# Gate/up of a two-layer encoder: where the second half's norm scales are spread, and three sums and products moved from GpSimd to VectorE

## The chip, the cores and the metric

The kernel runs on one core of a Trainium2 chip. A core has TensorE (PE, matrix products into PSUM), VectorE (DVE), ScalarE (ACT), GpSimd (POOL), and SyncE (SP), which here issues the DMA transfers. Each engine works through its own queue in order; semaphores tie the queues together. The metric is the device time of one execution in microseconds (us); less is better.

## The reference, cut to what matters

The reference is an encoder trunk of two layers over 1024 tokens of width 1024, all in fp32. The part that the change touches is the second half of each layer, the gated feed-forward:

```python
h = rms_norm(x, g_ffn[l]) * (1 + sc_f) + sh_f
gate, up = split_cols(h @ w_gu[l], (FFN_HIDDEN, FFN_HIDDEN))
x = x + gt_f * ((jax.nn.silu(gate) * up) @ w_down[l])
```

`FFN_HIDDEN` is 2816, so the gate and up matrices have 22 column blocks of 128 each. `rms_norm` divides each token by the root of the mean square of its 1024 features, so a token's scale is known only when all eight feature blocks of `x` are final.

## The kernel before, in words

**Tiling.** `x` lies transposed in SBUF: eight blocks `xt[:, k, :]` of 128 features by 1024 tokens (tiles `xb`, tags `x0` to `x7`). Tokens are taken in two halves of 512. Every fp32 factor is split into a high part (an fp32r copy by ACT) and a low part (the difference, by DVE or POOL), and a product is the sum of three matrix products of such parts (`mm3`, L202).

**Strassen-like products.** The 1024 by 256 weight columns of one step and the two halves of `h` are cut in 2 by 2, and seven products replace eight (`PRODUCTS`, L218: numbers 1, 2, 6, 5, 7, 3, 4, on operands `h11, h21, ht2, ht1, ht3, h22, ht4`). Each is 12 matmuls of 128x512 (`product`, L278). They accumulate in three PSUM banks per step: 1, 6, 7 and 4 in bank "a", 2 in "b", 5 and 3 in "c". Between two products of one bank ACT copies out what stands in it, so the second has to wait for that copy. `gu_product` (L1862) runs one product and what follows: ACT copies (`take`), DVE adds PSUM (`add`), and the gate's silu (ACT) or the multiplication by up (`done`).

**Steps.** There are 22 steps `q`, gate (even) and up (odd) in turn; two make a column block pair. The results of a pair lie in two tiles `sg`, which take the places of `x4` and `x5` for the first pair and `x6` and `x7` for the second (`gu_start`, L1942; `x_tile`, L1829). So the first results can be written only when the last reader of those blocks of `x` is through.

**The early loop.** Products 1 and 2 need only the first half of the tokens. The second half's norm is not ready when gate/up begins, so the first seven steps run products 1 and 2 first (`EARLY = 7`, L1956; the loop at L1994). In it `rstd_rows` (L458) is taken forward by two `next(norm)`: the first, at q = 0, sums the squares over features with PE and takes root and reciprocal; the second, at q = 1, spreads the scales over the partitions by four PE transposes into a PSUM tile `ps_r` (`spread`, L449) and returns it as `rows`. From q = 1 to 4, `t2_part` (L1961) multiplies two blocks of `x` by `rows` (`h_norm`, L1769) and makes `ht2` and `ht1`; `t3_part` and `t4_part` (L1978, L1983) make `ht3`, `h22` and `ht4`. All of that is DVE work with ACT copies between.

**The late loop** (L2017) then runs products 6, 5, 7, 3, 4 of steps 0 to 6, and all seven of the later steps. Weights come by DMA (`wr`, `gu_raw` L1832), are combined into sums (`ws`) by DVE and split (`wpt`) by ACT with DVE or POOL, up to eight ahead (`Ahead`, L261). The loads of step 1 and the sums use the places of `x0` to `x3`. The first ten splits are DVE's; after that DVE and POOL take turns.

**What sets the order.** Except for SP's queue, which is held in program order in the late loop (`pin`, L2016), the instructions are put in order for each engine by the compiler's planner: it takes the earliest in program order among those that its own clock holds ready. So an engine's order isn't the program's where a wait leaves room; in the trace, TensorE runs half of product 4 of step 0 ahead of product 3.

The line of the profile is always L49 (a wrapper that issues every instruction); instructions are told apart by the tiles they write and read.

Of the kernel before, what the change touches and what calls it, by code (L numbers as in the profile page):

```python
# [14 lines left out]
ALU = mybir.AluOpType  # L15
# [70 lines left out]
def trunk(ctx: ExitStack, tc, A, C, out):  # L86
    nc = tc.nc
    pe, act, dve, pool, sp = (
        Engine(tc, e) for e in (nc.tensor, nc.scalar, nc.vector, nc.gpsimd, nc.sync)
    )  # L90
# [187 lines left out]
    def product(num, banks, bank, a, b, m):  # L278
        if num in (1, 2, 5):
            banks[bank] = psl.tile([P, 512], F32, name="ps_w", tag="mm")  # L280
        ps = banks[bank]
        for k in range(m):
            mm3(
                ps, a[0][:, k], a[1][:, k], b[0][:, k], b[1][:, k],
                num in (1, 2, 5) and k == 0, k == m - 1, skip_group_check=True,
            )
        return ps
# [161 lines left out]
    def spread(r, j0, psp, tag="mm"):  # L449

        ps = psp.tile([P, 512], F32, name="ps_r", tag=tag)
        for j in range(4):
            pe.transpose(
                ps[:, j * P : (j + 1) * P], bc(r[:, j0 + j : j0 + j + 1], [P, P]), ident
            )
        return ps

    def rstd_rows(ssq, ntp, psp):  # L458

        r = rstd_cols([ssq], D, 4, ntp, psp)  # L460
        yield
        yield spread(r, 0, psp)
# [334 lines left out]
    rows = spread(rxs[1], 0, psl)  # L797
# [21 lines left out]
    for l in range(2):  # L819
# [175 lines left out]
        norm = {}  # L995
# [175 lines left out]
        for oc in range(NE, 8):  # L1171
            w = wab
            for half in range(2):
# [15 lines left out]
                i = 2 * (oc - NE) + half  # L1189
# [407 lines left out]
        for n in range(-AHEAD - 1, N + 1):  # L1597
# [44 lines left out]
            for end, (chunks, width) in norms.items():  # L1642
                if begins[end] <= m <= end and (m - begins[end]) % 8 == 7:
                    i = (m - begins[end]) // 8
# [150 lines left out]
        for i, n in enumerate((6, 7, 0, 1, 2, 3, 4, 5)):  # L1795
# [9 lines left out]
            if i == 1:  # L1805
                norm = rstd_rows(ssq, ntp, psl)
                next(norm)
            if i == 3:
                rows = next(norm)
# [22 lines left out]
        def gu_raw(q):  # L1832

            b, up = q // 2, q % 2
            c0 = up * FF + 2 * b * P
            raws = []
            for i in range(2):
                if q % 2:
                    t = x_tile(2 + i, [P, 4, 2 * P], "wr")
                else:  # L1840
                    t = wp.tile([P, 4, 2 * P], F32, name="wr", tag="wst", bufs=2)
                src = w_gu[:, c0 : c0 + 2 * P].rearrange("(k h p) n -> h p k n", h=2, p=P)
                sp.dma_start(t, src[i])
                raws.append(t)
            return raws
# [14 lines left out]
        sg, quads = {}, {}  # L1860

        def gu_product(q, p, a):  # L1862
            num, b, bank = p
            up = q % 2
            t = quads.setdefault(q, {})
            ps = product(num, t, bank, a, hb[b], 4)
            e, o = sg.get(q // 2, (None, None))
            lo, hi = slice(0, H), slice(H, S)

            def take(key, out=None):  # L1870
                if num == 1 and 5 <= q < EARLY:
                    out = spare[:, (q - 5) * H : (q - 4) * H]
                if out is None:
                    tag, bufs = ("u4", 1) if (q, num) == (4, 1) else ("u", 4)
                    out = ffp.tile([P, H], F32, name="u", tag=tag, bufs=bufs)
                t[key] = out
                act.copy(out, ps)

            def add(key):
                dve.tensor_tensor(out=t[key], in0=t[key], in1=ps, op=ALU.add)  # L1880

            def done(dst, src, eng=dve):
                if up:
                    eng.tensor_tensor(out=dst, in0=dst, in1=src, op=ALU.mult)
                else:
                    act.activation(dst, src, AF.Silu)

            if num == 1:
                take("11")
            elif num == 2:  # L1890
                add("11")
                if e is not None:
                    done(e[:, lo], t["11"], pool)
            elif num == 6:
                take("12", None if up else e[:, hi])
            elif num == 5:
                take("22", None if up else o[:, hi])
            elif num == 7:
                take("x")
                t22 = t["22"]  # L1900
                pool.tensor_tensor(out=t22, in0=t22, in1=t["x"], op=ALU.add)
                done(o[:, hi], t["22"], pool)
            elif num == 3:
                add("12")
                done(e[:, hi], t["12"], pool)
            else:
                done(o[:, lo], ps)
                if up:
                    steps.append(g_steps(q // 2, e, o))
# [3 lines left out]
        def g_steps(b, e, o):  # L1913


            b11, b12, b21, b22 = (t[:, i * H : (i + 1) * H] for t in (e, o) for i in range(2))

            def put(name, src):
                sp.dma_start(gpd[:, PLACE[name] + b, :], src)

            due = {
                3: lambda: [put(*a) for a in (("11", b11), ("22", b22), ("21", b21))],
                8: lambda: sub(b11, b12, b11),
                9: lambda: (sub(b12, b22, b12), sub(b22, b22, b11), put("t1", b11)),
                10: lambda: sub(b21, b21, b22),
                11: lambda: (put("t3", b12), put("t2", b22)),
                12: lambda: put("t4", b21),
            }
            return [due.get(i, lambda: None) for i in range(13)]
# [12 lines left out]
        def gu_start(b):  # L1942
            g_finish(1)
            sg[b] = [x_tile(4 + 2 * (b % 2) + i, [P, S], "sg") for i in range(2)]


        def first_cols(c0):
            rows = w_gu[:, c0 : c0 + P].rearrange("(k h p) n -> h p k n", h=2, p=P)
            return split_w(
                lambda v: [(v[:, 4 * i : 4 * i + 4], rows[i]) for i in range(2)], KC, eng=dve  # L1950
            )
# [9 lines left out]
        def t2_part(i, rows):  # L1961


            k = 2 * i
            for j in range(2):
                h_norm(k + j, 1, rows)
            b11, b12, b21, b22 = (
                xt[:, k + j, m * H : (m + 1) * H] for j in range(2) for m in range(2)
            )
            tag, bufs = ("ssq", 1) if i == 3 else ("sq", 2)  # L1970
            t2 = ntp.tile([P, H], F32, name="t2", tag=tag, bufs=bufs)
            sub(b11, b12, b11)
            shifted_sub(t2, b22, shift(k + 1), b11)
            h_split("t2", i, t2, dve)
            h_split("t1", i, b11, dve)
            return b12, b21, b22, t2

        def t3_part(i, b12, b21, b22, t2):  # L1978

            shifted_sub(b12, b22, dsh[:, i : i + 1], b12)  # L1980
            h_split("t3", i, b12, dve)

        def t4_part(i, b12, b21, b22, t2):  # L1983

            h_shift_split("22", i, b22, shift(2 * i + 1))
            shifted_sub(b21, b21, shift(2 * i + 1), t2)
            h_split("t4", i, b21, dve)
# [3 lines left out]
        rows = None  # L1991
        norm = rstd_rows(ssq, ntp, psl)
        ahead = Ahead(gu_parts())
        for q in range(EARLY):  # L1994
            for i in range(2):
                a = [w[:, 4 * i : 4 * i + 4] for w in early[q]]
                gu_product(q, PRODUCTS[i], a)
            if q + 4 < EARLY:
                early.append(first_cols((q + 4) % 2 * FF + (q + 4) // 2 * 2 * P))
            elif raw0 is None:  # L2000
                raw0 = gu_raw(0)
            if q == 0:
                next(norm)
            if q == 1:
                rows = next(norm)
            if 1 <= q < 5:
                bs.append(t2_part(q - 1, rows))
            if q == 1:
                t3_part(0, *bs[0])
                t4_part(0, *bs[0])  # L2010
            if q == EARLY - 2:
                ahead.fill(5)
# [4 lines left out]
        for q in range(NF):  # L2017
            if q % 2 == 0:
                gu_start(q // 2)
            if q < EARLY:  # L2020
                up = q % 2
                e = sg[q // 2][0][:, 0:H]
                if up:
                    pool.tensor_tensor(out=e, in0=e, in1=quads[q]["11"], op=ALU.mult)
            for i, p in enumerate(PRODUCTS[2 if q < EARLY else 0 :]):
                gu_product(q, p, ahead.get())
                if i == 1 and q < EARLY and not up:
                    act.activation(e, quads[q]["11"], AF.Silu)
                ahead.fill()
                g_step()  # L2030
                if q >= EARLY:
                    next(mods_due, None)
# [167 lines left out]
        for u in range(NU):  # L2200
            i, t = divmod(u, NB)
# [69 lines left out]
        norm = norm_half(odd, 1)  # L2271
# [91 lines left out]
```

## Time and profile before

| what | value |
|---|---|
| median of 3 runs | 2432.55 us (2431.05 to 2435.31) |
| the profiled execution's own time | 2435.83 us |
| its span, first to last instruction | 2434.1 us |
| PE busy | 2362.9 us (97%) |
| DVE busy | 1785.1 us (73%) |
| ACT busy | 1203.9 us (49%) |
| POOL busy | 759.6 us (31%) |
| mean granted TensorE clock | 0.991 |
| gate/up of layer 0, first product | at 589.09 us of the span |
| late loop of layer 0, first product | at 628.59 us |
| late loop of layer 1, first product | at 1815.16 us |

How to read it: the times in the rows of a timeline are from the start of the span. A row gives start, duration, engine, operation, the tile written and the tiles read, and in brackets how long the engine stood idle before it and what released it. With "x2" a row holds two instructions in a row. The end of a matmul is modelled, and matmuls overlap, so their pace is read from starts.

### The profile page before, as it was taken

The page shows a single profiled execution, that of the slowest core. Times are in us where ns is not written, and L with a number is a line of the kernel's source. Part 1 is how long each engine was busy: PE and PEld are TensorE (multiplying, and loading weights), DVE is VectorE, ACT ScalarE, POOL GpSimd, SP SyncE. Part 2 cuts the span into 40 slices and gives each one's busy share as a digit, 9 for nine tenths or more (in the row PEclk, how much of TensorE's full clock was granted, in tenths as well). Part 3 has the DMA queues.
Part 4 walks back from the last instruction along what each step waited for, and adds up shares of the span by engine and source line. Part 5 has one row for each costly group of instructions (what it writes and reads, how often), then busy time and mean ns, then how long its engine had stood idle before and what let it go on. Part 6 is the DMA issues. An engine that isn't in the chain of part 4 may idle for free.

```text
span 2434.1 us, 33735 instructions
## 1 busy us (share of the span) xinstructions
PE 2362.9 (97%) x11733; PEld 1963.3 (81%) x11733; DVE 1785.1 (73%) x2950; ACT 1203.9 (49%) x2290; POOL 759.6 (31%) x741
## 2 busy tenths in 40 slices
PE   8999999999999999999999999999999999999998
PEld 5778888788788788788787879987877888888886
DVE  5756899976967788586677589998787545547865
ACT  3421788954543333344543148887454333334443
POOL 1530344620244444300036114464004444430001
PEclk9999999999999999999999999999999999999999
DMA  8478215154245454596434861242534422329643
GB/s 262 151 237 269 61 27 148 43 181 148 87 143 178 156 183 150 166 276 195 144 96 113 277 187 27 58 125 68 191 96 136 142 100 96 103 101 305 206 129 108
DMA packets 305338, 356.98 MB, mean 147 GB/s; under 512 B 51964, under 2 KB 221788, under 8 KB 305168
## 3 DMA queue, kind: packets, MB, share of 16 engines
q1 hardware_dynamic: 283296, 342.07, 44.5%
q10 hardware_dynamic: 21504, 12.59, 2.0%
q8 instruction: 93, 1.52, 0.3%
q14 instruction: 77, 0.63, 0.1%
q0 software_dynamic: 368, 0.17, 0.0%
HBM read 269.79 MB, written 88.63 MB: 147 GB/s over the span
## 4 chain that ended last, share of the span: by engine, by line
PE 50%; DVE 4%; issue 4%; ACT 2%; POOL 1%; DMA 1%; ACTq 0%; SPq 0%; POOLq 0%; DVEq 0%
PE ps_w L49 21%; PE ps_d L49 14%; PE ps_o L49 3%; PE pv L49 2%; PE ps_ab L49 2%; PE ps_v L49 2%; PE T L49 2%; PE sC L49 2%; DMA qkd<-qko 1%; ACT pr L49 1%; PE ps_c L49 1%; POOL ct L49 1%; DVE pt L49 0%; PE ps_st L49 0%; DVE pr L49 0%
## 5 line engine op out<-in xcount | busy, mean ns | idle before, releaser
L49 PE MATMUL ps_d<-wpt 128*128 128x512 f32 x1848 | 424.3, 390 | 2.2 <-ACT wpt L49 1.9
L49 PEld LDWEIGHTS ps_d<-wpt 128*128 128x128 f32 x1848 | 345.6, 188 | 76.2 <-issue 3.0
L49 POOL TENSOR_SCALAR pr<-pr,rs 128x1024 f32<-128x1024 f32 (+2 forms) x248 | 192.8, 780 | 228.8 <-DVE rs L49 203.2
L49 POOL TENSOR_TENSOR sg<-sg,u 128x512 f32<-128x512 f32 x86 | 125.8, 1465 | 356.5 <-ACT sg L49 117.9
L49 PE MATMUL pv<-pt,vs 128*128 128x256 f32 x1088 | 182.5, 296 | 10.8 <-DVE y L49 3.6
L49 ACT CAST wpt<-w 128x512 fp32r<-128x512 f32 x154 | 95.7, 621 | 179.9 <-PE ps_d L49 161.4
L49 DVE TENSOR_TENSOR pt<-T,pt 128x512 fp32r<-128x512 f32 x272 | 178.2, 681 | 6.9 <-ACT pt L49 5.1
L49 PE MATMUL T<-identr,pr 128*128 128x128 f32 x1176 | 172.8, 273 | 1.0 <-DVE pt L49 0.5
L49 ACT CAST pt<-T 128x512 fp32r<-128x512 f32 x272 | 153.0, 586 | 37.8 <-PE T L49 35.8
L49 ACT COPY u<-ps_w 128x512 f32<-128x512 f32 x128 | 75.1, 587 | 193.1 <-PE ps_w L49 192.9
L49 POOL TENSOR_TENSOR wpt<-ws,wpt 128x512 fp32r<-128x512 f32 x80 | 112.3, 1405 | 179.0 <-ACT wpt L49 132.5
L49 DVE TENSOR_TENSOR wpt<-w,wpt 128x512 fp32r<-128x512 f32 x154 | 108.9, 707 | 80.6 <-ACT wpt L49 78.4
L49 PEld LDWEIGHTS pv<-pt,vs 128*128 128x128 f32 x1088 | 145.3, 189 | 27.6 <-DVE y L49 9.8
L49 PEld LDWEIGHTS T<-identr,pr 128*128 128x128 f32 x1176 | 138.2, 140 | 18.3 <-POOL pr L49 1.3
L49 DVE SCALAR_TENSOR_TENSOR acc<-wmt,condT,acc 128x512 f32<-128x512 f32 (+1 forms) x98 | 116.9, 1201 | 44.2 <-DMA wmt<-in_w_mod_dram 43.7
L49 ACT CAST wpt<-ws 128x512 fp32r<-128x512 f32 x176 | 107.7, 622 | 63.4 <-issue 28.2
L49 DVE TENSOR_TENSOR wpt<-ws,wpt 128x512 fp32r<-128x512 f32 x96 | 82.3, 868 | 62.9 <-ACT wpt L49 62.8
L49 DVE TENSOR_TENSOR wpt<-graw,wpt 128x512 fp32r<-128x512 f32 x154 | 109.2, 709 | 19.3 <-ACT wpt L49 19.3
L49 ACT CAST wpt<-graw 128x512 fp32r<-128x512 f32 x154 | 95.0, 617 | 48.2 <-DMA graw<-gpd 40.3
L49 DVE TENSOR_TENSOR ws<-wr 128x512 f32<-128x512 f32 x88 | 80.0, 911 | 49.2 <-POOL wpt L49 46.0
L49 PE MATMUL ps_w<-h22h,wpt 128*128 128x512 f32 x352 | 111.6, 399 | 4.3 <-ACT sg L49 3.6
L49 DVE TENSOR_REDUCE rs<-sC 128x1 f32<-128x1024 f32 x88 | 107.1, 1218 | 7.1 <-PE sC L49 5.2
(299 smaller groups left out, 6024.5 us busy)
## 6 DMA issues: line engine op xcount, KB each, us to landing
wr<-in_w_gu_dram SPq DMA_DIRECT2D x92, 512.0 KB, 4.1
gpd<-sg SPq DMA_DIRECT2D x154, 256.0 KB, 4.4
graw<-gpd SPq DMA_DIRECT2D x76, 512.0 KB, 3.5
w<-in_w_down_dram SPq DMA_DIRECT2D x110, 256.0 KB, 5.4
wmt<-in_w_mod_dram SPq DMA_DIRECT2D x48, 512.0 KB, 6.1
qk<-qkd SPq DMA_DIRECT2D x44, 512.0 KB, 6.7
wst<-in_w_o_dram SPq DMA_DIRECT2D x32, 512.0 KB, 3.9
wmt<-in_w_mod_dram SPq DMA_DIRECT2D x64, 256.0 KB, 3.8
```

The lines of the kernel that those rows point to most:

```text
L49: ins = op(*args, **kwargs)
```

## The change

The second `next(norm)` of the early loop moves from behind step 1's two products (and the load of a later step's first weights) to between them. And three elementwise operations of steps 0 and 1 (128x512 each) go to DVE in place of POOL: the sum that follows product 7 in steps 0 and 1 (`t22 + x`), and the multiplication of step 1's product "11" into `e`, the gate's silu. The same operations of steps 2 and on stay on POOL.

```diff
@@ gu_product
             elif num == 7:
                 take("x")
                 t22 = t["22"]
-                pool.tensor_tensor(out=t22, in0=t22, in1=t["x"], op=ALU.add)
+                (pool if q > 1 else dve).tensor_tensor(out=t22, in0=t22, in1=t["x"], op=ALU.add)
                 done(o[:, hi], t["22"], pool)
@@ early loop
             for i in range(2):
                 a = [w[:, 4 * i : 4 * i + 4] for w in early[q]]
                 gu_product(q, PRODUCTS[i], a)
+                if q == 1 and i == 0:
+                    rows = next(norm)
             if q + 4 < EARLY:
                 early.append(first_cols((q + 4) % 2 * FF + (q + 4) // 2 * 2 * P))
             elif raw0 is None:
                 raw0 = gu_raw(0)
             if q == 0:
                 next(norm)
-            if q == 1:
-                rows = next(norm)
             if 1 <= q < 5:
                 bs.append(t2_part(q - 1, rows))
@@ late loop
                 up = q % 2
                 e = sg[q // 2][0][:, 0:H]
                 if up:
-                    pool.tensor_tensor(out=e, in0=e, in1=quads[q]["11"], op=ALU.mult)
+                    (pool if q > 1 else dve).tensor_tensor(
+                        out=e, in0=e, in1=quads[q]["11"], op=ALU.mult
+                    )
```

## The prediction

> **What bounds the kernel now.** I read the page's first part, then the waits of TensorE over both gate/up stages, then the timelines of PE, DVE, ACT and POOL around those waits, and the granted clock there.
>
> ```profile
> span 2434.1 us, 33735 instructions
> PE 2362.9 (97%) x11733; PEld 1963.3 (81%) x11733; DVE 1785.1 (73%) x2950; ACT 1203.9 (49%) x2290; POOL 759.6 (31%) x741
> ```
>
> PE bounds the kernel as a whole, so the change can only win where PE stands or runs slowly. In layer 0's gate/up it stands three times (from 573 to 720 us), all at one place; layer 1 answers with the same three:
>
> ```profile
> PE ps_w L49 <- ACT sg L49: 2.6, 2, 1.8
> PE ps_w L49 <- ACT u L49: 0.9, 1, 0.9
> ```
>
> The PE timeline shows the place: the late products of step 0.
>
> ```profile
> 628.59 0.62 PE L49 MATMUL ps_w<-ht2h,wpt 128*128 128x512 f32 x2
> ...
> 631.31 0.69 PE L49 MATMUL ps_w<-ht1h,wpt 128*128 128x512 f32 x2
> ...
> 635.07 0.74 PE L49 MATMUL ps_w<-ht3h,wpt 128*128 128x512 f32 x2 [0.79 <-ACT sg L49]
> ...
> 639.05 0.72 PE L49 MATMUL ps_w<-ht4h,wpt 128*128 128x512 f32 x2 [0.92 <-ACT u L49]
> ...
> 642.26 0.73 PE L49 MATMUL ps_w<-h22h,wpt 128*128 128x512 f32 x2 [1.79 <-ACT sg L49]
> ...
> 648.33 0.39 PE L49 MATMUL ps_w<-ht2h,wpt 128*128 128x512 f32 x1
> ...
> 1815.16 0.62 PE L49 MATMUL ps_w<-ht2h,wpt 128*128 128x512 f32 x2
> ...
> 1836.08 0.40 PE L49 MATMUL ps_w<-ht2h,wpt 128*128 128x512 f32 x1
> ```
>
> One product takes 631.31 - 628.59 = 2.72 us at full pace. Five of them from 628.59 would let step 1 begin at 642.19; it begins at 648.33, 6.14 late. Layer 1: 1815.16 + 13.60 = 1828.76, in fact 1836.08, 7.32 late. So 13.46 us in both layers is all that a cure of this place can bring. Part of it is the clock (columns: window, length, busy us of PE, PEld, DVE, ACT, POOL, granted clock, DMA share, GB/s):
>
> ```profile
> 640.00:645.00 5.00, 3.21 (x12) 2.27 (x11) 4.91 (x6) 1.84 (x3) 2.16 (x2) 0.86 0.92 302
> 645.00:650.00 5.00, 5.00 (x19) 3.93 (x19) 4.16 (x8) 3.65 (x7) 0.00 (x0) 0.80 0.37 121
> 1827.00:1832.00 5.00, 3.21 (x9) 2.48 (x9) 4.88 (x7) 1.83 (x3) 1.72 (x2) 0.60 0.93 309
> 1832.00:1837.00 5.00, 5.00 (x17) 3.98 (x16) 3.08 (x6) 2.97 (x6) 0.00 (x0) 0.72 0.35 110
> ```
>
> Lost by it: 5 x (0.14 + 0.20) = 1.7 us in layer 0, 5 x (0.40 + 0.28) = 3.4 in layer 1. The rest is waiting.
>
> ACT is only the last link of those waits. Its copies into `sg` wait for DVE, the last reader of the blocks of `x` that `sg` replaces:
>
> ```profile
> 634.43 0.59 ACT L49 COPY sg<-ps_w 128x512 f32<-128x512 f32 x1 [0.64 <-DVE ht3l L49]
> 635.04 1.28 ACT L49 ACT_TABLE_LOAD   x1
> ...
> 641.62 0.59 ACT L49 COPY sg<-ps_w 128x512 f32<-128x512 f32 x1 [2.63 <-DVE ht4l L49]
> ```
>
> And DVE is behind from the moment the norm scales arrive:
>
> ```profile
> 596.72 0.17 DVE L49 RECIPROCAL rstd<-rstd 128x4 f32<-128x4 f32 x1
> 601.19 0.69 DVE L49 TENSOR_TENSOR u<-u,ps_w 128x512 f32<-128x512 f32 x1 [4.30 <-PE ps_w L49]
> 601.79 0.74 DVE L49 SCALAR_TENSOR_TENSOR xb<-xb,gsc,ps_r 128x512 f32<-128x512 f32 x1
> 602.45 1.22 DVE L49 TENSOR_TENSOR wlo<-wst,whi 128x1024 fp32r<-128x1024 f32 x1
> ...
> 633.06 1.89 DVE L49 TENSOR_TENSOR ht3l<-xb,ht3h 128x512 fp32r<-128x512 f32 x3
> ...
> 637.52 1.77 DVE L49 TENSOR_TENSOR ht4l<-xb,ht4h 128x512 fp32r<-128x512 f32 x1
> 639.21 1.78 DVE L49 SCALAR_TENSOR_TENSOR h22l<-xb,mod,h22h 128x512 fp32r<-128x512 f32 x1
> 640.91 0.68 DVE L49 TENSOR_TENSOR ht4l<-xb,ht4h 128x512 fp32r<-128x512 f32 x1
> ...
> 642.94 1.61 DVE L49 TENSOR_TENSOR ht4l<-xb,ht4h 128x512 fp32r<-128x512 f32 x1
> ...
> 646.69 0.69 DVE L49 TENSOR_TENSOR sg<-sg,ps_w 128x512 f32<-128x512 f32 x1 [0.81 <-PE ps_w L49]
> ...
> 647.90 2.49 DVE L49 TENSOR_TENSOR wpt<-ws,wpt 128x512 fp32r<-128x512 f32 x4
> ```
>
> It stands for 4.30 us, then works to 646 almost without a break, and the first split weights of step 1 come at 647.90, 0.43 before PE's 648.33. This queue sets the start of step 1; its length is what counts.
>
> **The change part by part.**
>
> *The spread.* These are the transposes, the start of the product that they would now precede, and POOL's operations at this place, and one row of SP's waits:
>
> ```profile
> 598.20 0.39 PE L49 MATMUL ps_w<-h21h,whi 128*128 128x512 f32 x1
> ...
> 600.92 0.60 PE L49 MATMUL ps_r<-identr,rstd 128*128 128x128 f32 x4
> ```
>
> ```profile
> 637.04 3.40 POOL L49 TENSOR_TENSOR sg<-sg,u 128x512 f32<-128x512 f32 x2 [114.17 <-DMA wr<-in_w_gu_dram]
> 642.29 1.72 POOL L49 TENSOR_TENSOR sg<-sg,u 128x512 f32<-128x512 f32 x1 [1.85 <-ACT sg L49]
> 653.53 3.00 POOL L49 TENSOR_TENSOR wpt<-ws,wpt 128x512 fp32r<-128x512 f32 x2 [9.53 <-ACT wpt L49]
> ...
> 658.19 1.74 POOL L49 TENSOR_TENSOR u<-u 128x512 f32<-128x512 f32 x1
> ```
>
> ```profile
> SPq L49 <- DVE ht4l L49: 5.1, 1, 5.1
> ```
>
> On PE nothing is added: four transposes go from 600.92 to 598.20, one product earlier. Their input, the reciprocal, ends at 596.89, 1.3 us before, so PE gets no new wait, and nothing behind it in PE's queue is delayed by more than it now is by the same transposes. `ps_r` ends at 598.80 instead of 601.52; it holds its PSUM bank 2.7 us longer at the front and is given up earlier behind. DVE, idle until 601.19, can begin the norms at about 598.9. At most it brings in 601.19 - 598.9 = 2.3 us of work; the two norms and their difference alone are 0.66 + 0.66 + 0.60 = 1.9 (steps between starts; 601.79 to 602.45 is a norm, 633.06 with three in 1.89 gives 0.60 for a difference). The lower bound is 0: if the planner leaves the sum of product 2 in front, the norms start where they do now. I take 2.1, since the order of now shows work taken forward whenever DVE is free. DMA loads gain from it, too: the load of step 1's weights goes to the place of `x3` and leaves SP's queue once an `ht4l` is through (the row of SP's waits), so it goes out as much earlier; nothing is added to that queue.
>
> *The multiplication into `e` and the sum of step 0.* In the POOL rows the first of the two at 637.04 is the former (the second, of step 3, stays) and 642.29 is the latter. On DVE each is 0.60. While POOL runs, DVE's own operations are stretched: 1.77, 1.78 and 1.61 against 0.68 and 0.74 undisturbed, 1.09 + 1.04 + 0.93 = 3.06 in three operations, one per POOL operation. Two of three go. From 637.52 to 647.90 DVE spends 10.38 us; less the 0.81 of idleness and the 3.06 that is 6.51 of work. After: 637.52 - 2.1 = 635.42, + 6.51, + 1.07 for the one stretch that stays, + 1.20 for the two new operations = 644.20; PE 0.43 later at 644.63. Bounds: if both are put behind the splits, 1.2 less; in-order waits are the last rival.
>
> *Does PE allow that?* Product 3 follows the `ht4l` of 640.91 by 1.35 us. That `ht4l` moves by 2.1 + 1.09, to 637.72 (638.32 if the multiplication stands ahead), so product 3 may begin at 639.07 to 639.67; it and the second half of product 4 are 18 matmuls, 4.08 us: PE is free at 643.15 to 643.75. So DVE remains the later of the two, with 644.63, and no single gap of PE is as long as the 1.79 of now. I take it that the clock then stays up.
>
> *The sum of step 1*, at 658.19, comes off POOL while DVE is busy with splits: + 0.60 and one stretch less. I cost it at nothing: the splits for step 2 are made on POOL from 653.53, and by the pace of PE they are needed 13.60 after 648.33, at 661.93, so 8.4 us later; with PE 3.7 us earlier 4.7 are left. If this cover were gone it would cost 0.6 per layer.
>
> *Sum.* Layer 0: 648.33 - 644.63 = 3.7 us. Layer 1 has the same DVE queue, 1186.57 later (1815.16 - 628.59): 1836.08 - (644.63 + 1186.57) = 4.9. Together 8.6; behind both places PE bounds, so the gain is carried to the end. Against the profiled execution's own time, 2435.83, this is 2427.2; that execution lies 3.28 above the median of the runs, 2432.55, from which I predict 2423.95, rounded 2424.0. Ends of the unknowns: PE's own limit, 643.15 in both layers, gives 5.2 + 6.4 = 11.6, 2421.0; a cure of the whole 13.46 would give 2419.1. With nothing from the spread, 2 x 2.1 is lost: a gain of 4.4, 2428.2.
>
> **The rivals.**
>
> *The early start is worth nothing.* The sums of products 1 and 2 (`u<-u,ps_w`) come at PE's pace. If DVE's order keeps one in front of the norms, it just waits earlier. For: the sum at 601.19 is where DVE waits now. Against: norms are independent of these sums. 2428.2, as worked out.
>
> *The clock drops all the same.* The rows show 0.86 to 0.60 after gaps of 1.79 us at most. If the shortened gaps still release it, or product 3 is put ahead of product 4 so that PE waits in one piece, PE loses 1.7 and 3.4 as now. Then step 1 begins at 643.45 (the middle of PE's bounds) + 1.7 = 645.15 and, in layer 1 by layer 0's count, at 643.45 + 3.4 = 646.85: gains of 648.33 - 645.15 = 3.2 and 1836.08 - (646.85 + 1186.57) = 2.7, 5.9 in all, 2426.7. For: it happens today in both layers. Against: less than 1 us is left of any single gap. [...]
>
> *Slower: the moved operations make DVE stand.* In DVE's order the multiplication waits for a silu behind the table load (1.28) and the sum for the copy that POOL now awaits for 1.85. On POOL that is free. On DVE it holds up the last `ht4l` and step 1's splits. With the early start used up by standing as well, the price is 2.1 + 1.28 + 1.85 = 5.23 per layer, 10.5 in both, against 8.6: 2434.5. It decides from 4.3 per layer; to be slower by over 0.2% PE would have to be held 6.7 per layer, which needs a reordering of the later splits too. For: DVE's queue is in order. Against: both come late in program order, so most likely are put behind the `ht4l`.
>
> **How the numbers follow.** The three runs lie within 4.3 us, so about 0.2%, 4.9 us, is what can be told from no change. Forecast: 0.52. No early start: 0.16, on the edge of that bound. Clock: 0.15, just beyond it. Moved operations in the way: 0.17. Faster by over 0.2% (under 2427.7): 0.50 of the forecast, 0.06 of the second case and 0.10 of the third, 0.66 together. Slower by over 0.2% (over 2437.4): 0.11 of the last case, where the later splits follow. Within: the remaining 0.23. The likeliest case's own range is 2421 to 2427. The range for 8 in 10 goes from 2419.5, near the full cure, to 2432.5, so that it leaves out the last rival alone.
>
> **What would show it.** Right: `ps_r` at about 598.2; DVE's idleness before the sum of product 2 gone; `ht4l` of step 0's blocks 3 us earlier; one POOL operation instead of three before the splits, and one stretched DVE operation; PE's third wait under 1 us; no clock under 0.95 in the windows; step 1 at 644 to 645 and 1830 to 1832. Wrong: DVE idle ahead of the multiplication or of the sum, PE waits elsewhere in the early loop for a PSUM bank that DVE gives up late, or new PE waits in steps 2 to 6.

## The result, and the profile after

The changed kernel takes 2423.65 us in the median of 8 runs, the kernel before 2432.93 in 8 runs beside them: a ratio of 0.9965 with a 95% interval of 0.9954 to 0.9976. Run once more beside another experiment it gave 0.9967 (0.9955 to 0.9980). The profiled execution after has a span of 2425.8 us against 2434.1.

```profile
span 2425.8 us, 33734 instructions
PE 2357.8 (97%) x11733; PEld 1959.7 (81%) x11733; DVE 1778.3 (73%) x2956; ACT 1202.4 (50%) x2290; POOL 745.1 (31%) x735
```

The waits of TensorE in the gate/up stage of layer 0 (573 to 720 us); layer 1 again has the same two rows:

```profile
PE ps_w L49 <- ACT u L49: 0.7, 1, 0.7
PE ps_w L49 <- ACT wpt L49: 0.6, 1, 0.6
```

The 3.5 us of three waits have become 1.3 us of two, and the second is a new one, for the weights of step 1. TensorE's timeline, in layer 0 and, in the last two rows, layer 1:

```profile
597.22 0.60 PE L49 MATMUL ps_r<-identr,rstd 128*128 128x128 f32 x4
...
627.61 0.62 PE L49 MATMUL ps_w<-ht2h,wpt 128*128 128x512 f32 x2
...
636.66 0.73 PE L49 MATMUL ps_w<-ht4h,wpt 128*128 128x512 f32 x2 [0.73 <-ACT u L49]
637.23 0.40 PE L49 MATMUL ps_w<-ht4l,wpt 128*128 128x512 f32 x1
637.47 0.62 PE L49 MATMUL ps_w<-h22h,wpt 128*128 128x512 f32 x2
...
642.98 0.51 PE L49 MATMUL ps_w<-ht2h,wpt 128*128 128x512 f32 x1 [0.56 <-ACT wpt L49]
...
1811.86 0.61 PE L49 MATMUL ps_w<-ht2h,wpt 128*128 128x512 f32 x2
...
1827.23 0.50 PE L49 MATMUL ps_w<-ht2h,wpt 128*128 128x512 f32 x1 [0.56 <-ACT wpt L49]
```

I call the time from the first late product of step 0 to the first of step 1 the stretch. It was 19.74 us in layer 0 and 20.92 in layer 1; it is 642.98 - 627.61 = 15.37 in both, with 13.60 at full pace. That is 4.4 and 5.5 us won, 9.9 together. Measured to the first late product of step 2 (657.01 against 627.61; before 661.98 against 628.59) it is 29.40 against 33.39 in layer 0 and 29.41 against 34.54 in layer 1: 4.0 + 5.1 = 9.1 us, since step 1 itself now takes 14.03 us and not 13.65. The two profiled executions differ by 8.3 us as a whole; what lies between is scattered over other stages, where the changed kernel has no other order of work (TensorE's order differs between the two at these places alone).

The clock no longer falls at either place (windows in the columns of the prediction):

```profile
635.00:640.00 5.00, 4.27 (x20) 3.17 (x19) 5.00 (x8) 3.36 (x7) 1.35 (x1) 1.00 0.62 202
640.00:645.00 5.00, 4.42 (x19) 3.13 (x17) 4.96 (x9) 3.29 (x7) 0.00 (x0) 1.00 0.64 211
1825.00:1830.00 5.00, 4.42 (x19) 3.12 (x18) 4.96 (x9) 3.80 (x7) 0.00 (x0) 1.00 0.49 167
```

VectorE's and GpSimd's timelines at the same place:

```profile
595.75 0.17 DVE L49 RECIPROCAL rstd<-rstd 128x4 f32<-128x4 f32 x1
597.86 1.41 DVE L49 SCALAR_TENSOR_TENSOR xb<-xb,gsc,ps_r 128x512 f32<-128x512 f32 x2 [1.93 <-PE ps_r L49]
...
600.68 0.69 DVE L49 TENSOR_TENSOR u<-u,ps_w 128x512 f32<-128x512 f32 x1 [0.16 <-PE ps_w L49]
...
635.09 1.29 DVE L49 TENSOR_TENSOR ht4l<-xb,ht4h 128x512 fp32r<-128x512 f32 x2
636.29 1.77 DVE L49 SCALAR_TENSOR_TENSOR xb<-xb,mod,t 128x512 f32<-128x512 f32 x1
...
638.59 0.68 DVE L49 TENSOR_TENSOR sg<-sg,u 128x512 f32<-128x512 f32 x1
...
639.79 0.68 DVE L49 TENSOR_TENSOR sg<-sg,u 128x512 f32<-128x512 f32 x1
...
642.96 2.50 DVE L49 TENSOR_TENSOR wpt<-ws,wpt 128x512 fp32r<-128x512 f32 x4
```

```profile
636.17 1.35 POOL L49 TENSOR_TENSOR sg<-sg,u 128x512 f32<-128x512 f32 x1 [114.27 <-ACT sg L49]
648.60 2.99 POOL L49 TENSOR_TENSOR wpt<-ws,wpt 128x512 fp32r<-128x512 f32 x2 [11.08 <-ACT wpt L49]
```

The 4.30 us of idleness ahead of the sum of product 2 have become 1.93 + 0.16. One operation is stretched to 1.77 in place of three. The sum of step 0 (638.59) and the multiplication (639.79) stand ahead of the splits, and VectorE doesn't stand for either. Which is which is told by ScalarE: the silu that needs the sum begins as the operation of 638.59 ends.

```profile
639.30 0.63 ACT L49 ACTIVATE sg<-sg 128x512 f32<-128x512 f32 x1 [0.58 <-DVE sg L49]
```

### The profile page after: what moved, and what is told of

The parts are those of the page before. It is cut to its first block, busy times and chain, and to the rows that moved or that the text cites. A ratio compares the mean times of both kernels' runs of the same rounds, so it can differ in the third digit from the quotient of the medians.

```text
span 2425.8 us, 33734 instructions
## 1 busy us (share of the span) xinstructions
PE 2357.8 (97%) x11733; PEld 1959.7 (81%) x11733; DVE 1778.3 (73%) x2956; ACT 1202.4 (50%) x2290; POOL 745.1 (31%) x735
## 4 chain that ended last, share of the span: by engine, by line
PE 48%; DVE 5%; issue 4%; ACT 2%; DMA 2%; POOL 1%; ACTq 0%; SPq 0%; POOLq 0%; DVEq 0%
PE ps_w L49 20%; PE ps_d L49 14%; PE ps_o L49 3%; PE pv L49 2%; PE T L49 2%; PE ps_v L49 2%; PE sC L49 2%; DMA qkd<-qko 1%; ACT pr L49 1%; PE ps_c L49 1%; POOL ct L49 1%; PE ps_ab L49 0%; DMA graw<-gpd 0%; DVE acc L49 0%; DVE pt L49 0%
## 5 line engine op out<-in xcount | busy, mean ns | idle before, releaser
L49 POOL TENSOR_TENSOR sg<-sg,u 128x512 f32<-128x512 f32 x82 | 116.5, 1422 | 357.7 <-ACT sg L49 228.5
L49 PE MATMUL sC<-qk 128*128 128x512 f32 x384 | 107.2, 401 | 4.8 <-ACT pr L49 4.8
```

Source lines behind the costliest of these rows:

```text
L49: ins = op(*args, **kwargs)
```

## The experiments

Two measures are taken from each profile: the stretch, and VectorE's lead-in, from the first late product of step 0 on TensorE to the first split of step 1's weights on VectorE (before 647.90 - 628.59 = 19.31, after 642.96 - 627.61 = 15.35). Times of whole runs differ by more than these amounts between executions, so where the two speak differently the profile is the finer measure. A kernel without a ratio was run once. The changed kernel's second profile gave the same stretches, 15.37 and 15.38.

| kernel | lead-in, layer 0 | stretch, layers 0 and 1 | to step 2, layers 0 and 1 | ratio to before |
|---|---|---|---|---|
| before | 19.31 | 19.74, 20.92 | 33.39, 34.54 | |
| before, again | 19.43 | 19.62, 19.71 | 33.45, 33.54 | |
| spread one step later | 19.98 | 20.00, 20.22 | 34.04, 34.24 | 1.0019 (1.0010 to 1.0028) |
| three operations moved, old spread | 17.30 | 17.00, 17.04 | 31.31, 31.33 | 0.9991 (0.9982 to 0.9999) |
| new spread alone | 16.35 | 16.50, 16.51 | 30.36, 30.39 | 0.9984 (0.9971 to 0.9997) |
| new spread, both sums moved | 15.87 | 16.50, 16.50 | 30.10, 30.10 | |
| new spread, multiplication moved | 15.79 | 15.38, 15.39 | 29.81, 29.84 | |
| after, sum of step 1 back on GpSimd | 15.35 | 15.37, 15.37 | 29.41, 29.41 | 0.9972 (0.9960 to 0.9984) |
| after | 15.35 | 15.37, 15.37 | 29.40, 29.41 | 0.9965 (0.9954 to 0.9976) |
| after, step 3's multiplication moved too | 14.81 | 14.65, 14.65 | 28.83, 28.89 | |
| after, spread inside product 1 | 14.74 | 14.32, 14.33 | 28.98, 28.99 | |
| both of these | 13.69 | 14.01, 14.00 | 27.94, 27.96 | 0.9952 (0.9939 to 0.9965) |

**The spread alone.** The three operations are put back on GpSimd:

```diff
-                (pool if q > 1 else dve).tensor_tensor(out=t22, in0=t22, in1=t["x"], op=ALU.add)
+                pool.tensor_tensor(out=t22, in0=t22, in1=t["x"], op=ALU.add)
...
-                    (pool if q > 1 else dve).tensor_tensor(
-                        out=e, in0=e, in1=quads[q]["11"], op=ALU.mult
-                    )
+                    pool.tensor_tensor(out=e, in0=e, in1=quads[q]["11"], op=ALU.mult)
```

> Only the spread is moved; the two sums and the multiplication stay on GpSimd. Measured by the stretch from the first late product of step 0 to the first of step 1 (before 19.74 us in layer 0 and 20.92 in layer 1, after 15.37 in both, 13.60 at full pace). Theory, by the terms of the prediction: 2.1 us of early start stay, all three stretched VectorE operations stay, no new ones: 16.8 us in both layers, 2.9 + 4.1 = 7 us less than before in all, about 1.4 more than after. Rival 'the moved operations are the cure': the stretch stays over 18.5 us and the time within 2.5 us of before. Rival 'the spread is everything': the same as after within 0.5 us of stretch. Clock: if it follows from long gaps, no half-speed piece in the stretch.

Measured: 16.50 and 16.51, as the theory has it within 0.3. All the stretched operations are there again (VectorE's rows, two operations in the first; then TensorE's waits):

```profile
635.77 3.46 DVE L49 TENSOR_TENSOR ht4l<-xb,ht4h 128x512 fp32r<-128x512 f32 x2
...
640.58 1.61 DVE L49 TENSOR_TENSOR ht4l<-xb,ht4h 128x512 fp32r<-128x512 f32 x1
```

```profile
PE ps_w L49 <- ACT sg L49: 1.6, 1, 1.6
PE ps_w L49 <- ACT u L49: 0.7, 1, 0.7
```

The clock stays up in both layers, though one wait of 1.6 remains: in layer 0 three matmuls behind it take 641.39 - 640.70 = 0.69 us, against 0.68 at full pace, and layer 1 has the same two waits and a stretch of 16.51. Over whole runs this kernel is 4.2 us faster than before in the median, less than the 7 that were expected; the interval of the ratio, 0.7 to 7.1 us, still holds them.

**The three operations alone.** The spread goes back behind both products:

```diff
-                if q == 1 and i == 0:
-                    rows = next(norm)
...
+            if q == 1:
+                rows = next(norm)
             if 1 <= q < 5:
```

> Only the three operations go to VectorE; the spread stays behind both products of step 1. Theory: no early start, two stretched operations fewer, two operations more: 18.1 us of stretch in both layers, 1.6 + 2.8 = 4.4 us less than before, if the clock stays up; 18.1 plus 1.7 or 3.4 where it drops. Rival 'the spread is everything': 19.7 to 20.9 as before, time within 1 us of before. Rival 'the moved operations make VectorE stand': stretch over 21 us, slower than before by 2 us or more, VectorE idle ahead of the multiplication or of step 0's sum.

Measured: 17.00 and 17.04, a good 1 us better than the theory, and no wait of VectorE ahead of the moved operations. The clock stays up, as the theory took it: behind the last of the waits three matmuls take 644.81 - 644.13 = 0.68 us, and layer 1 has the same waits within 0.1 us. Of the 1.1 us, 0.4 is a shorter lead-in (17.30 against 18.1 - 0.43 = 17.67) and 0.7 is the 0.43 between the first split and TensorE: here TensorE begins 0.30 ahead of that split. The third wait of TensorE, 1.79 before, is 0.69. Over whole runs the kernel is 3.6 us faster in the median, 4.4 were expected.

```profile
637.23 0.73 PE L49 MATMUL ps_w<-ht3h,wpt 128*128 128x512 f32 x2 [0.79 <-ACT sg L49]
...
641.21 0.73 PE L49 MATMUL ps_w<-ht4h,wpt 128*128 128x512 f32 x2 [0.95 <-ACT u L49]
...
643.33 0.73 PE L49 MATMUL ps_w<-h22h,wpt 128*128 128x512 f32 x2 [0.69 <-ACT sg L49]
```

So in the one profile of each, each half of the change by itself keeps the clock. (That it always does isn't shown: with the spread alone a wait of 1.6 us was left, and the last section has a drop behind 1.53 us of idleness.) And their gains don't add up: to step 2 of layer 0 the spread brings 3.03 us and the operations 2.08, both together 3.99 and not 5.11; in layer 1 it is 4.15 and 3.21 against 5.13. The whole runs are too coarse to show that.

What is counted twice, 1.1 and 2.2, is for the most part one wait of VectorE in the kernel before, ahead of the sum of product 3: 0.81 us in layer 0 (at 646.69) and 1.92 in layer 1.

```profile
646.45 0.63 PE L49 MATMUL ps_w<-ht4l,wpt 128*128 128x512 f32 x1
...
1834.36 0.69 DVE L49 TENSOR_TENSOR sg<-sg,ps_w 128x512 f32<-128x512 f32 x1 [1.92 <-PE ps_w L49]
```

The half clock accounts for this wait: product 3 took from 642.26 to 646.45, 4.19 us, and 5.28 in layer 1, where the half clock lasted 6.83 us against 3.41. At the full pace of 2.72 it would have ended 1.47 and 2.56 us earlier, which is more than the wait. In the kernels with either half of the change the wait is gone, and it can go only once. Without it the lead-in before is 18.5 us in both layers and in both profiles; from there the spread takes 2.1 (16.35), the operations 1.2 (17.30), and both 3.1 (15.35), which nearly adds up.

**The spread later still.** It goes behind the first product of step 2, and all that uses it moves by one step:

```diff
-                if q == 1 and i == 0:
+                if q == 2 and i == 0:
                     rows = next(norm)
...
-            if 1 <= q < 5:
-                bs.append(t2_part(q - 1, rows))
-            if q == 1:
+            if 2 <= q < 6:
+                bs.append(t2_part(q - 2, rows))
+            if q == 2:
```

> As after, but the spread comes one step later than before, behind the first product of step 2 (and what uses it one step later). Theory (the start of VectorE's queue sets the start of step 1): VectorE's norms begin 2.7 us later than in the kernel before and 5.4 later than after, so the stretch is 18.1 + 2.1 to 2.7 = 20.2 to 20.8 us, plus clock; time at or up to 4 us over before. Rival (VectorE makes the delay good by filling its idle time, or another limit lies close by): stretch as in the run with the moved operations alone, 18 us or less, time 4 us under before.

Measured: lead-in 19.98, stretch 20.00 and 20.22, 3.65 us slower than before in the median. This is the other side of the first experiment: one product later than in the kernel with the operations alone costs 19.98 - 17.30 = 2.7 us of lead-in, the length of a product, so on balance VectorE makes nothing good; 1.07 of it is a wait of VectorE's own. The stretch is at the lower end of the expected 20.2 to 20.8 or just under it, although the clock dropped. TensorE's first wait (for the copy that an `ht3l` holds up) is now the longest, and half clock is back: in layer 0 the next three matmuls take 641.70 - 640.25 = 1.45 us, against 0.68 at full pace, and layer 1, with the same waits, has a stretch of 20.22. Here alone VectorE stands ahead of a moved operation, the sum of step 0, for the copy of product 5, as in the prediction's last rival:

```profile
640.25 1.22 PE L49 MATMUL ps_w<-ht3h,wpt 128*128 128x512 f32 x2 [2.57 <-ACT sg L49]
```

```profile
646.32 1.41 DVE L49 TENSOR_TENSOR sg<-sg,u 128x512 f32<-128x512 f32 x1 [1.07 <-ACT sg L49]
```

**The sum of step 1 back on GpSimd.** Its condition becomes `q > 0`:

```diff
-                (pool if q > 1 else dve).tensor_tensor(out=t22, in0=t22, in1=t["x"], op=ALU.add)
+                (pool if q > 0 else dve).tensor_tensor(out=t22, in0=t22, in1=t["x"], op=ALU.add)
```

> As after, but the sum of step 1 stays on GpSimd. Theory (its cost is hidden by the splits made ahead): the stretch 15.4 us as after, no new wait of TensorE behind it, time within 1 us of after. Rival (it matters, since VectorE is busy there): up to 1.1 - 0.6 = 0.5 us per layer slower than after, seen as a wait of TensorE in steps 1 to 3.

Measured: 15.37 in both layers and 29.41 to step 2, as after; TensorE has the same two waits. That operation's place is without effect here, as the cover of splits made ahead implied.

**The multiplication alone, and the sums alone,** each with the new spread. In the first both sums stay on GpSimd, in the second the multiplication does (the lines are those of the first experiment).

> The spread as after; of the three operations only the multiplication of step 1 is on VectorE, both sums stay on GpSimd. So far the stretch from the first late product of step 0 to that of step 1 was 16.50 us with the spread alone and 15.37 after. Theory (VectorE's queue is the limit, each GpSimd operation stretches one of its operations by 0.9 to 1.1 us, each one taken over costs it 0.60): against after the sum's stretch of 0.93 comes back and its 0.60 goes: 15.7 us in both layers. Rival (the sum of step 0 alone carries the gain): 16.3 us or more.

> The spread as after; both sums are on VectorE, the multiplication of step 1 stays on GpSimd. Theory: against after 1.09 of stretch comes back and 0.60 goes: 15.9 us in both layers. Rival (the multiplication, being ahead of the last readers of x, carries no gain on VectorE): 15.4 us or less.

By the stretch both miss: 15.38 with the multiplication, as after, and 16.50 with the sums, as with neither. So both rivals fall, the one that gave the whole gain to the sum of step 0 and the one that gave the multiplication none, and by this measure the multiplication has all of it. With it on GpSimd the second `ht4l` of VectorE ends 10.94 us after the first late product, with it on VectorE after 8.76; TensorE's wait of 1.6, for the copy that this `ht4l` holds up, is there in the first case only, and it sets the 16.50. By VectorE's lead-in the theory holds: from 16.35 the multiplication takes 0.56, the sums 0.48, both 1.00, which is their sum within 0.04. The expected amounts were 0.49 and 0.33. The stretch hides the sum's part because TensorE starts step 1 on ACT's high parts and is held up by the low ones two matmuls later: with the multiplication alone step 1 takes 14.43 us, after 14.03, 13.60 at full pace. GpSimd's row of the first kernel holds the multiplication of step 3 and the sum of step 0 back to back, and VectorE has two stretched operations for it, of which the second is no longer a reader of `x`:

```profile
635.39 3.04 POOL L49 TENSOR_TENSOR sg<-sg,u 128x512 f32<-128x512 f32 x2 [114.28 <-ACT sg L49]
```

```profile
635.51 1.77 DVE L49 SCALAR_TENSOR_TENSOR xb<-xb,mod,t 128x512 f32<-128x512 f32 x1
637.21 1.77 DVE L49 TENSOR_TENSOR ws<-wr 128x512 f32<-128x512 f32 x1
```

**Further the same way.** The spread is issued inside product 1 of step 1, behind its ninth matmul (`product` gets a function to call after `k == 2`), and step 3's multiplication goes to VectorE as well; then each by itself:

```diff
+            if between and k == 2:
+                between()
...
-                    (pool if q > 1 else dve).tensor_tensor(
+                    (pool if q > 3 else dve).tensor_tensor(
                         out=e, in0=e, in1=quads[q]["11"], op=ALU.mult
                     )
```

> As after, but the spread stands inside product 1 of step 1, behind its ninth matmul, and the multiplication of step 3 is on VectorE, too. Theory: VectorE's norms begin 3 matmuls, 0.68 us, earlier, and the last stretched operation loses its 1.07 for 0.60 of own work: 1.15 less in VectorE's queue, so the stretch would be 14.2 us; TensorE's own wait for the copy between products 7 and 4 (0.73 after, plus its restart) sets a floor of about 14.5 us. So 14.5 us, 0.9 per layer or 1.8 us in all less than after. Rival (the planner puts product 3 straight behind 7 and TensorE waits there in one piece): stretch 15 us or more, perhaps with half clock, no better than after.

> The changed kernel once more, for the comparison with the run beside it: stretch 15.37 us in both layers, 0.996 to 0.998 of the time of the kernel before.

> As after, but the spread stands inside product 1 of step 1, behind its ninth matmul; the multiplication of step 3 stays on GpSimd. Together with that multiplication on VectorE the stretch was 14.0 us, after 15.37. Theory (both parts shorten VectorE's queue, by 0.68 and by 0.47): 14.7 us. Rival (the earlier spread does it alone, since it also changes TensorE's order to 7, 3, 4 without a wait): 14.0 us.

> As after, but the multiplication of step 3 is on VectorE, too, so that GpSimd has nothing to do before the splits. Theory: a stretch of 1.07 goes and 0.60 is added: 14.9 us. Rival (this last stretched operation costs nothing, since TensorE's own wait between products 7 and 4 is as late): 15.3 us or more.

Measured: alone 14.32 and 14.65, with lead-ins 0.61 and 0.54 shorter than after (0.68 and 0.47 were expected), so each part shortens VectorE's queue by about what was expected. By the stretch the earlier spread lies between its theory, 14.7, and its rival, 14.0; step 3's multiplication is better than its theory, 14.9, and its rival, 15.3, falls. Together 14.01, better than the 14.5 of the theory: the floor that I saw in TensorE's wait between products 7 and 4 isn't one. In this kernel the planner puts product 3 straight behind 7, `h22` is ready by then, and no wait of TensorE is left between 573 and 720 us. It takes 2421.72 us, the changed kernel beside it 2424.97, the kernel before 2433.06. By the ratios, 0.9952 (0.9939 to 0.9965) against 0.9967 (0.9955 to 0.9980), it is faster than before; that it is faster than the change isn't shown by the times, since the intervals overlap. By the profile it is 1.46 us per layer ahead at step 2, 2.9 in all, about the 3.25 between the medians.

**The kernel before once more,** for the clock.

> The kernel before once more, for the clock. If half speed is released by how much TensorE stands within one window of 3.41 us of a grid that lies anew in every execution, the waits are the same 0.79, 0.92 and 1.79, but the stretch is 18.0 us where no window holds enough of them, 19.7 with one window at half speed and up to 21 with two. If half speed belongs to the place, 19.7 and 20.9 come again.

Measured: the same three waits; stretches of 19.62 and 19.71, with a piece at half speed in each layer (a granted clock of 0.66 in one window of 5 us, so 1.7 us lost, in each). Layer 1 had a longer piece in the first profile (0.60 and 0.72 in two windows) and here has a shorter one at the same place:

```profile
1825.00:1830.00 5.00, 2.43 (x10) 1.36 (x8) 5.00 (x5) 2.37 (x5) 3.34 (x2) 1.00 0.31 97
1830.00:1835.00 5.00, 4.83 (x14) 3.85 (x15) 3.84 (x6) 2.56 (x6) 1.71 (x1) 0.66 0.67 224
```

The drop came in four of four layers with these waits, so a case without it wasn't seen; its length isn't tied to the place. With the two short waits of after it came in none of the eight layers profiled (after twice, the sum of step 1 back, the multiplication alone: stretches of 15.37 to 15.39). The layer 1 stretch of 20.92 in the first profile, and 1.2 us of the gain there, were thus partly the luck of one execution.

## Why the prediction was right

*The time.* 2424.0 was forecast, 2423.65 measured; the gain, 8.6, was 9.3 between the medians and 9.1 at step 2 of the two layers. That the times agree within 0.4 us is luck: the median of the kernel before was 2431.24 to 2433.06 beside the three larger sets of runs, and against its second profile the gain at step 2 is 4.1 + 4.1 = 8.2.

*The queue of VectorE sets the start of step 1.* Right in the main. The forecast put the first split at 644.20, a lead-in of 15.61; it was 15.35. Every experiment that shortened or lengthened this queue moved the lead-in by about the time by which it did so: 2.7 us for a product of delay, 0.6 for a quarter of one, 0.5 for an operation taken over. But the queue reaches TensorE in two places: through the last readers of `x`, which hold up product 3, and through the weights. With the spread alone and with both sums moved the first of them set the start of step 1, 16.50, whatever the lead-in.

*The spread, 2.1 us.* Right in size: idleness went from 4.30 to 2.09, and against the kernel with the operations alone the lead-in is 17.30 - 15.35 = 1.95 shorter.

*The multiplication and the sum of step 0: two stretches of three gone, 1.20 of own work.* 3.06 - 1.07 - 1.20 = 0.79 was forecast, 1.00 measured. They stand ahead of the splits, as assumed, and VectorE doesn't wait for them.

*The sum of step 1, nothing.* Right.

*The 0.81 of idleness.* The forecast took this wait of VectorE out of its sum without a reason. It did go, since product 3 no longer ran late and at half clock; in layer 1, where the forecast took the queue to be the same, it was 1.92.

*The sum over the layers.* 3.7 and 4.9 were forecast for the start of step 1, 4.4 and 5.5 measured. The term that was mis-sized is the 0.43 us between the first split and TensorE: it is 0.02 after. Before, it was no wait for splits: the three waits all lie earlier, and TensorE was still at its own product 4, late by the clock. After, TensorE is there first and begins as soon as ACT has copied a high part. Most of that comes back at once, for step 1 takes 0.38 us longer than before. I had taken step 1 to run at full pace once begun, and it waits for splits on the way.

*TensorE's waits.* The first vanished and the third did, too; I expected less than 1 us of it. The wait for weights, 0.56, wasn't forecast. TensorE's order changed only in that product 3 now comes after a quarter of product 4 instead of about half.

*The clock.* It stayed up, as assumed; that step was argued from 'no single gap as long as now', and this reason is too simple. With the spread alone a wait of 1.6 us and one of 0.7 were left, and the clock stayed up in both layers; elsewhere in the kernel before a drop follows two waits of 0.77 and 0.76 us (the last section has it).

*The rivals.* 'The early start is worth nothing' falls by the two runs with and without it. 'The clock drops all the same' falls: the half clock came in four of four layers with the long waits and in none of eight with the short ones, so at this place it came with the waits. 'VectorE stands for the moved operations' was seen, but only with the spread put off by two products.

## What to carry to other kernels

Where the busiest engine waits at a seam, follow the wait to the engine whose queue is full there, and ask when that queue could have begun: one product earlier was worth more here than taking operations off it. An operation on GpSimd wasn't free for VectorE here: each stretched one of VectorE's by 0.9 to 1.1 us while doing the same on VectorE itself costs 0.6, so at a place where VectorE's queue is the limit the 'idle' engine was the dearer one. And when two cures each end the same wait (here one that half clock had made), their gains overlap; measure them apart before adding them.

## What the runs showed of the hardware

Between 100 and 2400 us TensorE's granted clock is 1.00 or 0.50 in the profiles before and after, and the pieces at 0.50 are 3.41 us long, one of them 6.83. In each profile their starts lie on one grid of 3.41 us: in the kernel before 643.60 - 131.60 = 512.00 is 150 times 3.4133, and 793.78 - 643.60 = 150.18 is 44 times. The two grids lie differently, 1.89 us and 0.27 us behind a whole multiple of 3.4133 us from the start of the span. This is every such piece, with TensorE's idleness in the 3.41 us ahead of it, and for each kernel the stretch of the grid with the most idleness that no piece follows:

| kernel | start of the piece, us | its length, us | idleness of TensorE in the 3.41 us ahead, us |
|---|---|---|---|
| before | 131.60 | 3.41 | 1.73 |
| before | 643.60 | 3.41 | 1.79 |
| before | 793.78 | 3.41 | 2.65 |
| before | 1305.78 | 3.41 | 1.70 |
| before | 1401.35 | 3.41 | 1.53 |
| before | 1828.02 | 6.83 | 1.90 |
| before | none at 257.9 | | 1.42 |
| after | 788.75 | 3.41 | 2.65 |
| after | 1631.84 | 3.41 | 0.00 |
| after | none at 133.41 | | 1.53 |

The 1.53 us at 1401.35 are two waits of 0.77 and 0.76; the 1.53 at 133.41 are one wait. So the same amount stands once with a piece behind it and once without, and no limit can be read from these two profiles. The second half of the longer piece, at 1831.43, follows 0.82 us. The piece at 1631.84 follows no idleness at all; it lies in the attention stage, and in the 3.41 us ahead of it stand sixteen `ps_st` matmuls with an output of one column, 1.84 us in all. Why it came isn't shown.

The pieces at 793.78 and 788.75 lie in a stage that the change doesn't touch. In the runs of the kernel before that stand beside the later experiments, 2429.23 us came with a mean granted clock of 0.994 and 2437.14 with 0.991. By my estimate 0.003 of 2435 us is about 7 us, most of the 7.9 between the two, so the half clock can be a part of the spread between runs of one kernel.
